# Every second chunk of an input matrix: the low half of a float32 split completed by an adding DMA instead of GpSimd

## The chip, the core and the metric

The kernel runs on one core of one Trainium2 chip. The metric is the device time of one execution in microseconds (us), given as the median of several runs. In the text, PE is TensorE, DVE is VectorE, ACT is ScalarE, POOL is GpSimd and SP is SyncE, which here only issues DMAs. "L120" is line 120 of the kernel before.

## The reference

One decoder block over 512 positions of 1024 channels, all in float32. Two token mixers (a gated depthwise convolution of 31 taps, and a gated linear recurrence) run on slices of one wide projection; their outputs are merged by sigmoid gates, and a SwiGLU layer follows. Cut to what matters:

```python
h = rmsnorm(x, norm1_g)                     # 512 x 1024
z = h @ w_in + b_in                         # w_in: 1024 x 6656
z_glu, z_rx, z_rg, z_ga, z_gb = split(z, [2048, 3328, 4608, 5632])
u = z_glu[:, :1024] * sigmoid(z_glu[:, 1024:])
u = silu(layernorm(causal_depthwise_conv(u, conv_dw_w, conv_dw_b)))
y_a = u @ conv_w_out + conv_b_out
xb = causal_depthwise_conv(z_rx, lru_conv_w, lru_conv_b)
y_b = (rg_lru(xb, ...) * gelu(z_rg)) @ lru_w_out
x = x + (sigmoid(z_ga) * y_a + sigmoid(z_gb) * y_b) @ w_mix_out
x = x + (silu(h2 @ ffn_w1) * (h2 @ ffn_w3)) @ ffn_w2       # h2 = rmsnorm(x, norm2_g)
return rmsnorm(x, norm_f_g)
```

The change concerns the second line alone, the product with `w_in`.

## The kernel before, in words

**Products.** Each float32 matrix is split into two parts in the rounded format float32r: a high part h = round(v) and a low part l = v - h. A product is then three TensorE matmuls, high by high, high by low and low by high (`mm3`). Operands lie channels by positions, so that a product of one 128-column chunk of `w_in` with all 512 positions is 8 blocks of 128 input channels times 3, that is 24 matmuls of 128x128 by 128x512, into one PSUM bank of 512 float32 per partition.

**Weight chunks.** `w_in` is cut into 52 chunks of 128 columns (512 KB each). The list `chunks` holds them, the ten gate chunks of the recurrence and all later weights in the order of use. `emit_chunk` makes one: it takes one of `RAW = 4` buffers (`raw`), lets SP load the chunk into it, takes one of `HL = 5` pairs of buffers (`hl`, high part in the first half, low part in the second), and splits. `weights(key)` emits chunks until `AHEAD = 4` beyond the one asked for. A `raw` buffer comes free when its split is done; an `hl` pair comes free when PE has read it.

**The split before.** `split_to` has ACT copy the chunk to the high part (L124, a rounding copy), and then POOL subtract it from the chunk into the low part (L120). For the first two `w_in` chunks VectorE does the rounding and POOL or VectorE the subtraction. Later weights (`lo=vec`) are subtracted by VectorE.

**The order.** `ORDER` lists the steps of this stage: `u` (two chunks, the gated convolution's input), `rx`, `rg`, `gb`, `ga` (one chunk each), `g` (two small products for the recurrence's gates, 8 or 12 matmuls, L868) and `r` (a scan, no matmul). So the first steps `u0 u1 rx0 rx1 gb0 rx2 u2` hold chunks 1 to 10. Beside these steps `run_beside` spreads the depthwise convolution on VectorE (L743, 240 instructions with one tap each) and then the layer norm, whose two column sums are a pair of matmuls each (`column_mean`, L754). `make_out_sums` lets POOL form sums of later weights (`ows`), which are loaded and stored through SP in the same stage. What each engine executes is its own queue in order; outside the blocks marked `manual_schedule` (the start of this stage and two short places later) a planner with estimated durations orders each queue at compile time, and semaphores hold the instructions at run time. PSUM has six banks for the products of this stage (`psum`); a bank comes free when ACT or VectorE has read it.

**Adding transfers before.** There is one such place: `f_sum` for two of the SwiGLU sums (L363), where POOL issues a DMA that adds one buffer onto another in SBUF.

Of the kernel before, what the change touches and what calls it, by code (L numbers as in the profile page):

```python
# [8 lines left out]
F32 = mybir.dt.float32  # L9
F32R = mybir.dt.float32r  # L10
AF = mybir.ActivationFunctionType
ALU = mybir.AluOpType

P = 128
# [12 lines left out]
ND = D // P  # L27
# [11 lines left out]
FEW, MANY = 32, 112  # L39

LAG = 12

# [43 lines left out]
def tile_block(ctx, tc, a, out):  # L88
# [25 lines left out]
    vec, act, pe, pool_e = nc.vector, nc.scalar, nc.tensor, nc.gpsimd  # L114
# [4 lines left out]
    def sub(eng, o, x, y):  # L119
        return eng.tensor_tensor(out=o, in0=x, in1=y, op=ALU.subtract)  # L120

    def split_to(h, l, full, eng, copy=act.copy):

        copy(h, full)  # L124
        if eng is vec and "tie" in newest:
            with tc.issue_after(newest["tie"]):
                last = sub(eng, l, full, h.bitcast(F32))
        else:
            last = sub(eng, l, full, h.bitcast(F32))
        if eng is pool_e:  # L130
            newest["sub"] = last.ins
        return h, l, last

    def split(name, full, eng, p_=None, copy=act.copy):
        p_ = p_ or pairt(name)
        return split_to(*p_, full, eng, copy)[:2]


    chunks = []
    held = {}  # L140
    emitted = [0]

    def wchunk(key, src, kt, cols, where="hl", lo=pool_e, after=None):
        chunks.append((key, src, kt, cols, where, lo, after))
# [13 lines left out]
    def emit_chunk(copy=act.copy, lo_by=None):  # L158
        if emitted[0] == GATES_AT:
            load_gates()  # L160
        key, src, kt, cols, where, lo, after = chunks[emitted[0]]
        emitted[0] += 1
        lo = lo_by or lo
        n = kt * cols
        if where == "made":
            raw = src()
        else:
            raw = raws.tile([P, 1024], F32, tag="raw", name=f"raw_{key}")
        rv = raw[:, :n]
        if where == "made":  # L170
            pass
        elif callable(src):
            src(raw)
        else:
            newest["load"] = nc.sync.dma_start(rv.rearrange("p (k n) -> p k n", k=kt), src).ins
        if where != "long":
            hl = hls.tile([P, 2, 1024], F32R, tag="hl", name=f"hl_{key}")
            h, l, _ = split_to(hl[:, 0, :n], hl[:, 1, :n], rv, lo, copy)
            if after:
                after(rv, h)  # L180
            held[key] = (h.rearrange("p (k n) -> p k n", k=kt), l.rearrange("p (k n) -> p k n", k=kt))
        else:
            held[key] = [
                split_to(longt(f"{key}h{i}", F32R), longt(f"{key}l{i}", F32R), rv[:, i * T : (i + 1) * T], lo)
                for i in range(2)
            ]

    def emit_to(n, copy=act.copy, lo_by=None):
        while emitted[0] < min(len(chunks), n):
            emit_chunk(copy, lo_by)  # L190
# [5 lines left out]

    w_in = a["w_in"][0].rearrange("(k p) n -> p k n", p=P)

    def w_in_chunk(m):
        wchunk(f"in{m}", w_in[:, :, m * P : (m + 1) * P], ND, P)  # L200

    GLU, RX, RG, GA, GB = 0, 16, 26, 36, 44
    pieces = gate_pieces()
# [8 lines left out]
    def load_gates():  # L212
      with tc.issue_after(newest["load"]):
        for gi, name in enumerate(("lru_wa", "lru_wx")):
            nc.sync.dma_start(gate_rows[:, gi, :], a[name][0].rearrange("h r n -> (h r) n"))
# [29 lines left out]
    for kind, j in ORDER:  # L245
        if kind == "g":
            gate_chunk(j)
        elif kind == "u":
            w_in_chunk(GLU + j)
            w_in_chunk(GLU + 8 + j)  # L250
        elif kind != "r":
            w_in_chunk({"rx": RX, "rg": RG, "gb": GB, "ga": GA}[kind] + j)
# [218 lines left out]
    def row_at(c):  # L471
        b = sum(c >= s_ for s_ in starts) - 1
        return b + (c - starts[b]) // P, (c - starts[b]) % P

    at, col, parts = 0, {}, []
    for name, n in ROWS:
# [4 lines left out]
        while done < n:  # L481
            m = min(n - done, P - row_at(at + done)[1])
# [189 lines left out]
    with tc.manual_schedule(engines={ET.PE, ET.Activation, ET.DVE, ET.SP}):  # L672
# [23 lines left out]
        _, ws, ps = early[0]  # L696
# [34 lines left out]
    def beside():  # L731
# [18 lines left out]
        def column_mean(name, tot, scale):  # L750

            ps = bank2(f"{name}p")
            for i, v in enumerate(tot):
                pe.matmul(ps, onesr, v, start=i == 0, stop=i == 1)  # L754
            act.activation(ps, ps, AF.Copy, scale=scale)
            return ps

        def pause(n):
            for _ in range(n):
                yield  # L760
# [6 lines left out]
        tot = split("lnms", tot, vec)  # L767
        yield from pause(LAG)
        mean = column_mean("lnm", tot, 1.0 / DC)
# [10 lines left out]
        tot = split("lnvs", tot, vec)  # L780
        yield from pause(LAG)
        rs = column_mean("lnv", tot, 1.0 / DC)
# [599 lines left out]
```

## Time and profile before

| | |
|---|---|
| median of 3 runs | 795.95 us (795.84 to 796.22) |
| span of the profiled execution, first to last instruction | 794.7 us, 1.25 us under the median |
| busy: PE | 786.6 us (99%), 4300 matmuls |
| busy: DVE, ACT, POOL | 688.9 us (87%), 473.8 us (60%), 221.9 us (28%) |
| granted TensorE clock | 1.00 throughout |
| DMA queues | 135.32 MB by SP's hardware queue, 1.05 MB by POOL's software queue |
| the 52 loads of `w_in` chunks | issued between 3.0 and 282.0 us, 512 KB each |

The profile gives for each instruction its engine, line, operands by name, start and duration, and what ended the engine's idle time before it. The stage of the change lies between some 25 and 320 us. The chain of work that ended last is followed back from the last instruction; where it stays on one engine, that engine was not waiting for another. DMA share is the mean busy share of the core's 16 DMA engines.

### The profile page before, as it was taken

What the parts mean: (1) busy time and instruction counts of PE and PEld (TensorE: products, weight loads), DVE (VectorE), ACT (ScalarE), POOL (GpSimd) and SP (SyncE); (2) the same over time, 40 slices, a digit from 0 to 9 for tenths busy, and PEclk for the clock granted to TensorE, in tenths of its full rate; (3) what the DMA queues carried; (4) which work ended last, traced back from release to release, by engine and by line L of the source; (5) the groups of instructions that cost most, each with busy time, mean ns of one, the idle gap of its engine ahead of it and who ended that gap; (6) DMA issues with size and microseconds to landing.
All of it is one profiled execution on the core that took longest, in us unless ns stands there. A gap on an engine that the chain in (4) does not pass through costs nothing.

```text
span 794.7 us, 12042 instructions
## 1 busy us (share of the span) xinstructions
PE 786.6 (99%) x4300; PEld 686.4 (86%) x4300; DVE 688.9 (87%) x1047; ACT 473.8 (60%) x695; POOL 221.9 (28%) x174
## 2 busy tenths in 40 slices
PE   8999999999999999999999999999999999999997
PEld 8888888888888888888888898999999999888886
DVE  6699899999989988786887889979888888989867
ACT  7645685987768855563335575545455555585544
POOL 1865766797666856030000000000000000000000
PEclk9999999999999999999999999999999999999999
DMA  7955646487564664359847545655333332686552
GB/s 209 247 145 145 193 139 206 121 247 208 170 206 138 206 189 119 129 192 276 271 159 247 173 133 159 182 152 164 114 108 107 106 106 81 200 287 201 186 172 106
DMA packets 184603, 137.14 MB, mean 173 GB/s; under 512 B 14259, under 2 KB 163167, under 8 KB 184543
## 3 DMA queue, kind: packets, MB, share of 16 engines
q1 hardware_dynamic: 184255, 135.32, 56.3%
q0 software_dynamic: 288, 1.05, 0.7%
q8 instruction: 34, 0.56, 0.3%
q14 instruction: 26, 0.21, 0.1%
HBM read 113.79 MB, written 18.64 MB: 167 GB/s over the span
## 4 chain that ended last, share of the span: by engine, by line
PE 92%; DMA 3%; DVE 3%; ACT 1%; issue 0%; SPq 0%; ACTq 0%; POOLq 0%; DVEq 0%
PE z L544 35%; PE or L1003 12%; PE yb L544 7%; PE ft L1141 7%; PE fa L1141 7%; PE ya L544 5%; PE mxr L1003 5%; PE fr L1141 3%; PE g L868 3%; PE fb L1141 2%; PE fe L1151 2%; PE f L544 1%; DMA raw_fb<-raw_fb 1%; PE fe L1152 1%; DMA raw_fb<-in_ffn_w_dram 1%; PE f L1175 1%
## 5 line engine op out<-in xcount | busy, mean ns | idle before, releaser
L743 DVE SCALAR_TENSOR_TENSOR cv<-u,par,cv 128x511 f32<-128x511 f32 (+19 forms) x240 | 162.4, 731 | 6.0 <-ACT cv L740 5.7
L120 POOL TENSOR_TENSOR hl_in<-raw_in,hl_in 128x1024 fp32r<-128x1024 f32 x50 | 121.1, 2427 | 73.7 <-ACT hl_in L124 67.8
L120 POOL TENSOR_TENSOR ows<-ows 128x256 f32<-128x256 f32 x66 | 56.5, 858 | 37.9 <-DMA ows<-in_ffn_w_dram 34.9
L124 ACT CAST hl_ft<-raw_fb 128x1024 fp32r<-128x1024 f32 x40 | 41.9, 1050 | 31.7 <-DVE raw_fb L365 14.8
L124 ACT CAST hl_in<-raw_in 128x1024 fp32r<-128x1024 f32 x50 | 52.0, 1043 | 12.7 <-PE z L544 6.6
L120 DVE TENSOR_TENSOR hl_ft<-raw_fb,hl_ft 128x1024 fp32r<-128x1024 f32 x40 | 48.6, 1220 | 9.4 <-ACT hl_ft L124 9.4
L363 POOL DMA_DIRECT2D raw_fb<-raw_fb x2 | 1.9, 928 | 158.1 <-DVE raw_fb L365 158.1
L120 DVE TENSOR_TENSOR hl_fb<-raw_fb,hl_fb 128x1024 fp32r<-128x1024 f32 x30 | 36.7, 1223 | 8.4 <-ACT hl_fb L124 8.0
L544 PE MATMUL z<-h10h,hl_in 128*128 128x512 f32 (+1 forms) x106 | 41.1, 388 | 0.2 <-DVE h10l L600 0.2
L544 PE MATMUL z<-h12h,hl_in 128*128 128x512 f32 (+1 forms) x106 | 40.6, 384 | 0.0
L544 PE MATMUL z<-h14h,hl_in 128*128 128x512 f32 (+1 forms) x106 | 40.6, 384 | 0.0
L544 PE MATMUL z<-h17h,hl_in 128*128 128x512 f32 (+1 forms) x106 | 40.6, 384 | 0.0
L544 PE MATMUL z<-h11h,hl_in 128*128 128x512 f32 (+1 forms) x106 | 40.6, 383 | 0.0
L544 PE MATMUL z<-h16h,hl_in 128*128 128x512 f32 (+1 forms) x106 | 40.6, 383 | 0.0
L544 PE MATMUL z<-h13h,hl_in 128*128 128x512 f32 (+1 forms) x106 | 40.6, 383 | 0.0
L544 PE MATMUL z<-h15h,hl_in 128*128 128x512 f32 (+1 forms) x106 | 40.6, 383 | 0.0
L365 DVE TENSOR_TENSOR raw_fb<-raw_fb,raw_fb 128x1024 f32<-128x1024 f32 x28 | 34.2, 1222 | 7.0 <-DMA raw_fb<-in_ffn_w_dram 6.7
L124 ACT CAST hl_fb<-raw_fb 128x1024 fp32r<-128x1024 f32 x30 | 31.4, 1047 | 8.6 <-PE mxr L1003 3.7
L124 ACT CAST hl_ob<-raw_ob 128x1024 fp32r<-128x1024 f32 (+1 forms) x23 | 23.3, 1015 | 19.6 <-PE or L1003 10.5
L120 DVE TENSOR_TENSOR hl_ob<-raw_ob,hl_ob 128x1024 fp32r<-128x1024 f32 (+1 forms) x23 | 27.1, 1176 | 6.3 <-ACT hl_ob L124 4.4
L1141 PE MATMUL ft<-hs_1h,hl_ft 128*128 128x256 f32 x160 | 30.4, 284 | 0.0
L124 ACT CAST hl_ot<-raw_ot 128x1024 fp32r<-128x1024 f32 (+1 forms) x17 | 17.5, 1027 | 17.8 <-PE or L1003 16.8
(1082 smaller groups left out, 2630.7 us busy)
## 6 DMA issues: line engine op xcount, KB each, us to landing
raw_in<-in_w_in_dram SPq DMA_DIRECT2D x52, 512.0 KB
raw_fb<-in_ffn_w_dram SPq DMA_DIRECT2D x96, 256.0 KB
ows<-in_ffn_w_dram SPq DMA_DIRECT2D x44, 256.0 KB
os<-ows SPq DMA_DIRECT2D x22, 512.0 KB
raw_ob<-in_ffn_w_dram SPq DMA_DIRECT2D x33, 256.0 KB
raw_ot<-os SPq DMA_DIRECT2D x33, 256.0 KB
raw_lo<-in_lru_w_out_dram SPq DMA_DIRECT2D x16, 320.0 KB
x<-in_x_dram SPq DMA_DIRECT2D x16, 256.0 KB
```

What stands on the lines that cost most here:

```text
L120: return eng.tensor_tensor(out=o, in0=x, in1=y, op=ALU.subtract)
L124: copy(h, full)
L363: pool_e.dma_start(out=q, in_=y, accum_op=ALU.add)
L365: vec.tensor_tensor(out=q, in0=q, in1=y, op=ALU.add)
L544: pe.matmul(ps, l, r, start=i == 0, stop=i == n - 1)
L743: vec.scalar_tensor_tensor(out=acc[c][:, s:], in0=u[c][:, : T - s], scalar=dw(c, s), in1=acc[c][:, s:], op0=ALU.mult, op1=ALU.add)
L868: pe.matmul(ps, l, r, start=k == 0, stop=k == len(mms) - 1)
L1003: pe.matmul(banks[i], l_[:, ts], r_, start=start and n == 0, stop=stop and n == 2, skip_group_check=again)
L1141: pe.matmul(ps[:, HALVES[i]], lw[:, 4 * i + c, :], rx_, start=not (again or i or c or m), stop=bool(i and c == 3 and m == 2), skip_group_c ...
L1151: pe.matmul(ps, h[:, 4 * i + c, :], both_[c], start=c == 0, stop=False, skip_group_check=True)
L1152: pe.matmul(ps[:, LO], l[:, 4 * i + c, :], xh, start=False, stop=c == 3, skip_group_check=True)
L1175: pe.matmul(plain_1[:, cs], l, r, start=k == 0 and m == 0, stop=k == ND - 1 and m == 2)
```

## The change

`w_in` chunks are counted as they are listed. Of the 52, those with an even number from 6 on (6, 8, ..., 52: 24 chunks) are split in another way: ACT writes the negated rounded chunk into the low part, POOL issues a DMA that adds the chunk onto it (so that the low part is v - round(v)), and ACT then rounds the chunk into the high part. The other 28 chunks are split as before.

```diff
+TRANSFERS_FROM = 6
...
+    def split_by_transfer(h, l, full):
+
+        act.activation(l, full, AF.Copy, scale=-1.0)
+        last = pool_e.dma_start(out=l.bitcast(F32), in_=full, accum_op=ALU.add)
+        act.copy(h, full)
+        return h, l, last
...
         if where != "long":
             hl = hls.tile([P, 2, 1024], F32R, tag="hl", name=f"hl_{key}")
-            h, l, _ = split_to(hl[:, 0, :n], hl[:, 1, :n], rv, lo, copy)
+            parts_ = hl[:, 0, :n], hl[:, 1, :n], rv
+            h, l, _ = split_by_transfer(*parts_) if lo == "transfer" else split_to(*parts_, lo, copy)
...
+    n_in = [0]
+
     def w_in_chunk(m):
-        wchunk(f"in{m}", w_in[:, :, m * P : (m + 1) * P], ND, P)
+        n_in[0] += 1
+        by_transfer = n_in[0] >= TRANSFERS_FROM and n_in[0] % 2 == 0
+        wchunk(f"in{m}", w_in[:, :, m * P : (m + 1) * P], ND, P, lo="transfer" if by_transfer else pool_e)
```

## The prediction

> **What bounds the kernel now.** I read the busy times, then the chain that ended last, then busy time by stretch.
>
> ```profile
> PE 786.6 (99%) x4300; PEld 686.4 (86%) x4300; DVE 688.9 (87%) x1047; ACT 473.8 (60%) x695; POOL 221.9 (28%) x174
> ```
>
> The chain in order of time (start, length, what; x counts matmuls):
>
> ```profile
> 25.24 43.59 PE z L544 x192
> ...
> 118.85 2.76 PE g L868 x12
> ...
> 134.34 21.78 PE z L544 x96
> 156.12 1.85 PE g L868 x8
> 157.96 21.78 PE z L544 x96
> ...
> 243.37 65.30 PE z L544 x288
> 308.68 0.45 PE lnmp L754 x2
> ...
> 374.86 25.16 PE ya L544 x111
> ```
>
> Busy us (and instructions) of PE, PEld, DVE, ACT, POOL, then granted clock, DMA share, GB/s:
>
> ```profile
> 0.00:25.00 25.00, 22.40 (x160) 21.43 (x161) 16.08 (x46) 19.52 (x45) 6.29 (x10) 1.00 0.81 226
> 25.00:320.00 295.00, 295.00 (x1302) 244.11 (x1301) 275.44 (x416) 202.27 (x256) 207.02 (x159) 1.00 0.60 176
> 700.00:795.00 95.00, 89.38 (x402) 73.95 (x400) 78.77 (x123) 53.62 (x87) 0.00 (x0) 1.00 0.56 180
> ```
>
> The reader is to see three things. In the whole stage of the change (25 to 320 us) PE is busy 295.00 of 295.00 us, and the chain never leaves it. PE idles 2.6 us before that stage and 5.6 us at the kernel's end, and no edited chunk is used in either. And a matmul goes at the same pace whether POOL works or not: 21.78/96 = 227 ns beside POOL, 25.16/111 = 227 ns in the ya stage, where POOL has no split to do. So work taken from POOL cannot shorten PE's row; the question is only whether a chunk, a PSUM bank or a column sum now comes late.
>
> **The change part by part.** Prices, from rows grouped by form, the queue table, a window of the only adding transfers, and two waits (total us, times, longest):
>
> ```profile
> L120 POOL TENSOR_TENSOR hl_in<-raw_in,hl_in 128x1024 fp32r<-128x1024 f32 x50 | 121.1, 2427 | 73.7 <-ACT hl_in L124 67.8 <-issue 2.9 <-DMA raw_in<-in_w_in_dram 1.2
> L124 ACT CAST hl_in<-raw_in 128x1024 fp32r<-128x1024 f32 x48 | 49.9, 1043 | 12.3 <-PE z L544 6.6 <-DMA raw_in<-in_w_in_dram 4.3 <-issue 1.1
> L124 ACT CAST hl_gate<-raw_gate 128x512 fp32r<-128x512 f32 x10 | 6.1, 614 | 7.3 <-POOL ows L120 3.2 <-POOL hl_in L120 2.3 <-PE z L544 1.8
> L624 ACT ACTIVATE x<-x,stats 128x512 f32<-128x512 f32 x2 | 1.4, 724 | 0.6 <-DVE stats L568 0.6
> L363 POOL DMA_DIRECT2D raw_fb<-raw_fb x2 | 1.9, 928 | 158.1 <-DVE raw_fb L365 158.1
> ```
>
> ```profile
> q0 software_dynamic: 288, 1.05, 0.7%
> ```
>
> ```profile
> DMA to landing us min/median/max: 4.7/5.3/6.0
> ```
>
> ```profile
> 498.00:506.00 8.00, 8.00 (x69) 8.00 (x68) 8.00 (x13) 5.07 (x8) 1.00 (x1) 1.00 0.49 108
> ```
>
> ```profile
> ACT hl_in L124 <- DMA raw_in<-in_w_in_dram: 4.7, 3, 3.8
> ```
>
> ```profile
> SPq L175 <- POOL hl_in L120: 38.7, 19, 6.5
> ```
>
> *POOL, removed:* 24 subtractions of 2.43 us, 58.2 us; *added:* 24 issues of 0.93 us, 22.3 us. POOL goes from 207.0 to some 171 busy us. It is not on the chain: gain nothing.
>
> *ACT, added:* one negating copy of 128x1024 for each chunk. No row shows it. Its like is L624, a scaled copy of 512 columns in 724 ns; 512 more columns cost 1043-614 = 429 ns in the rounding copies, so 1.15 us. Ends: 1.04 us (as the rounding copy) and 1.45 us (twice L624); I take 1.15, as L624 is the same kind of instruction. L624's row has no table load beside it, so none is counted. 24 x 1.15 = 27.6 us, ACT from 202.3 to 229.9 of 295 us. In sum it is hidden under PE; where it is not is worked out below.
>
> *DMA, added:* the two transfers of before took 0.7% of 794.7 us on 16 engines, 2.8 us each; 24 of them are 67 us, and the stage's share goes from 0.60 to 0.83. That leaves room on the average, less in bursts.
>
> *The chunk's own delay.* Before: 1.04 + 2.43 and 0.08 between them, 3.55 us. Now 1.15 + 0.93 + 5.3 = 7.4 us until the low part is there (landing counted from the issue's end, the worse reading); the high part's rounding runs beside the transfer. So the low part comes 3.8 us later, and the raw buffer comes free 3.8 us later. The load behind it waits that long in SP's queue, where such waits exist already (38.7 us in 19), and what stands behind it with it: the ext copies for the gates, the loads and stores of ows. ACT waited for raw_in only 4.7 us in all, because loads wait in full buffers for a free hl pair; 3.8 us come out of that reserve. For the ext copies one row: the last piece for a gate product is issued at 110.54, and the product begins at 118.85, 8.3 us for one copy.
>
> Now the chunks with the least time, from the timeline (start, length, [idle before it]):
>
> ```profile
> 26.18 1.99 ACT L124 CAST hl_in<-raw_in 128x1024 fp32r<-128x1024 f32 x2
> ...
> 139.41 0.62 ACT L124 CAST xb5h<-xb 128x512 fp32r<-128x512 f32 x1 [6.22 <-DVE xb L821]
> 139.94 1.05 ACT L124 CAST hl_in<-raw_in 128x1024 fp32r<-128x1024 f32 x1
> ...
> 152.99 1.05 ACT L124 CAST hl_in<-raw_in 128x1024 fp32r<-128x1024 f32 x1
> ...
> 178.29 0.59 ACT L124 CAST y2h<-z 128x512 fp32r<-128x512 f32 x1 [2.26 <-DVE z L906]
> ...
> 248.76 1.04 ACT L124 CAST hl_in<-raw_in 128x1024 fp32r<-128x1024 f32 x1
> ```
>
> ```profile
> 27.30 4.75 POOL L120 TENSOR_TENSOR hl_in<-raw_in,hl_in 128x1024 fp32r<-128x1024 f32 x2 [0.55 <-ACT hl_in L124]
> ...
> 141.06 2.99 POOL L120 TENSOR_TENSOR hl_in<-raw_in,hl_in 128x1024 fp32r<-128x1024 f32 x1 [6.72 <-ACT hl_in L124]
> ...
> 154.12 2.81 POOL L120 TENSOR_TENSOR hl_in<-raw_in,hl_in 128x1024 fp32r<-128x1024 f32 x1
> ...
> 249.88 2.40 POOL L120 TENSOR_TENSOR hl_in<-raw_in,hl_in 128x1024 fp32r<-128x1024 f32 x1 [4.57 <-ACT hl_in L124]
> ```
>
> ```profile
> 110.54 0.53 SPq L848 DMA_DIRECT2D ext3l<-xb4l  x1
> ```
>
> A chunk is 24 matmuls, 5.44 us, and its third matmul (0.45 us in) is the first to need a low part. By ORDER the 96 matmuls from 134.34 are rx6, rg1 and the two chunks of u5; the second of these, chunk 24, begins at 134.34 + 16.33 = 150.67 and needs the low part at 151.12. ACT rounds it at 139.94. Now: negated by 141.1, issued by 142.0 (POOL was idle), landed at 147.3: 3.8 us to spare. Chunk 26 (gb3) is the second of the 96 from 157.96: needed at 163.85. ACT, busy without a gap since 139.41, comes 1.15 us later to it: 154.14, negated 155.3, issued 156.2, landed 161.5: 2.3 us to spare, the least of all. Chunk 42 (gb7), the fourth from 243.37, is needed at 260.14: 248.76, 249.9, 250.8, landed 256.1: 4.0 us. Chunk 6, the first by transfer, is rounded at 27.1, issued at some 30.6 behind POOL's work, landed at 35.9, needed at 25.24 + 16.33 + 0.45 = 42.0.
>
> So the landing time decides: chunk 26 makes PE wait from 7.6 us on, 24 from 9.1, 42 from 9.3. The row's 5.3 us were measured at a DMA share of 0.49; here it is higher:
>
> ```profile
> 25.00:35.00 10.00, 10.00 (x47) 8.29 (x46) 4.67 (x19) 5.94 (x7) 8.36 (x4) 1.00 1.06 260
> ...
> 145.00:155.00 10.00, 10.00 (x46) 8.29 (x45) 9.94 (x16) 9.79 (x14) 8.67 (x9) 1.00 0.38 111
> 155.00:165.00 10.00, 10.00 (x45) 8.25 (x45) 10.00 (x16) 9.90 (x14) 9.11 (x7) 1.00 0.64 192
> 165.00:175.00 10.00, 10.00 (x46) 8.29 (x45) 9.27 (x15) 9.89 (x14) 9.71 (x9) 1.00 0.90 261
> ```
>
> Lower end 4.7 us; upper end 8.1, if the 2.8 us of engine time double beside loads. At 5.3 PE waits 0; at 8.1 it waits 0.5 us, at chunk 26. I take 0.25. [...] The two transfers before ran beside loads at a share of 0.49 and do not decide it.
>
> **Sum:** -0 (POOL) + 0.25 (chunk 26) = +0.25 us: the profiled span from 794.7 to 794.95, the median, 1.25 us above it, from 795.95 to **796.2 us**. Changes under 0.2% (1.6 us) I call no change, about what a measurement of this kernel can tell.
>
> **The rivals.**
>
> *A. Landings of 12 us,* twice the longest seen, because software transfers and loads crowd (0.90 of the engines from 165 to 175 us before the change, 1.06 at 25 to 35). Then chunk 6 lands at 42.6, 0.6 us late; chunk 24 at 154.0 against 151.12 + 0.6, 2.3 late; chunk 26 at 168.2 against 163.85 + 2.9, 1.5 late; chunk 42 at 262.8 against 260.14 + 4.4, in time. Together 4.4 us on 795.95: 800.4 us. Against it: the share 0.38 at 145 to 155, and no landing over 6.0. It decides from some 9.5 us, where chunks 26 and 24 together cost 1.9 us.
>
> *B. ACT's backlog.* From 139.41 to some 176 ACT has no gap (9.79, 9.90, 9.89 of 10), and chunks 24, 26, 28 and 30 fall there: 4 x 1.15 = 4.6 us late before the gap at 178.29. PE's banks are freed by ACT, or by DVE behind ACT. With no slack PE would wait 4.6 us, with 1.6 us of it 3.0: 799.0 us. For it: those windows. Against it: DVE is as full there (9.94, 10.00), and ACT itself had waited 6.22 us for it, so DVE more than ACT sets when banks are freed. It decides from a slack under 3 us.
>
> *C. The planner's queues come out otherwise.* This stage is not ordered by hand, and new durations can move any instruction. The place with a number is the layer norm's first sum:
>
> ```profile
> L120 DVE TENSOR_TENSOR lnmsl<-lnmt,lnmsh x1: 1160/1160/1160, 304.6 to 304.6; 128x512 fp32r<-128x512 f32 x1
> ```
>
> It ends at 305.8, and PE needs it with the second matmul from 308.68, some 3.1 us later. Five negating copies put ahead of it on ACT (5 x 1.15 = 5.8 us) would make PE wait 2.7 us: 798.7 us.
>
> *D. Faster.* DVE is 93% busy in the stage, and some of it is waiting for POOL:
>
> ```profile
> L120 DVE TENSOR_TENSOR xb9l<-xb,xb9h 128x512 fp32r<-128x512 f32 x1 | 2.3, 2337 | 0.0
> L120 DVE TENSOR_TENSOR y7l<-z,y7h 128x512 fp32r<-128x512 f32 x1 | 0.7, 694 | 0.0
> ```
>
> An equal operation takes 694 ns with one input in PSUM and up to 2337 with both in SBUF, 1.6 us more, less than one POOL subtraction. [...] Half the subtractions gone frees a few us of DVE. But the end moves only if PE's idle time does: 5.6 us in the last 95, which this stage does not feed. If a shifted queue saved 2 us of them: 794.0 us.
>
> **How the numbers follow.** No change to be measured, as summed: 0.60. A 0.12, B 0.12, C 0.10: slower, 0.34. D 0.06. The likeliest gives 796.2, its own range 795.7 to 797.0. For 8 in 10 I reach from 795.2 to 800.5: this leaves out D and half of A, 0.12, and some of the likeliest's own edge.
>
> **What would show it.** Right: PE busy 295 of 295 us in the stage; 24 POOL issues near 0.9 us, and landings under 7.6; the negating copy near 1.15 us; ACT near 230, POOL near 171 us, DMA share near 0.83. Wrong: gaps in PE before z at chunk 24, 26 or 42 with the DMA as releaser (A), with ACT or DVE as releaser at 140 to 180 us (B), before lnmp (C), or fewer than 5.6 idle us after 700 (D). A negating copy that brings table loads, or an issue that holds POOL far above 0.93 us, would void the sum.

## The result, and the profile after

The changed kernel takes **807.8 us** (median of 4 runs, 806.5 to 810.7) against 796.0 (795.8 to 796.2): 1.0151 times as long, 95% interval 1.0139 to 1.0163. It is slower by 11.8 us where no change was forecast (796.2, range 795.2 to 800.5). The profiled execution took 806.5 us, the shortest of the four, with a span of 804.5 against 794.7; so 9.8 of the 11.8 us are seen in the profile. The medians and ratios of this document are those of fast executions; one execution of a later experiment (`from14`) took 1313.9 us at a mean granted clock of 0.557 and is left aside.

The busy times of the changed kernel:

```profile
PE 789.8 (98%) x4300; PEld 686.8 (85%) x4300; DVE 688.0 (86%) x1047; ACT 498.7 (62%) x721; POOL 183.7 (23%) x174
```

The parts cost about what they were said to cost: ACT 24.9 us more, POOL 38.2 less, and PE's work is the same. Its new operations, by form, and the landing times of the 24 transfers:

```profile
L142 ACT ACTIVATE hl_in<-raw_in 128x1024 fp32r<-128x1024 f32 x24 | 25.3, 1053 | 2.1 <-PE z L557 1.2 <-DMA raw_in<-in_w_in_dram 0.9
DMA to landing us min/median/max: 4.5/6.3/8.0
```

The time went where PE waits. Two names recur: g5, g6 and so on are the small gate products, and the ext copies gather, from a neighbouring `xb`, the rows that such a product also needs; some are made by ACT, the others by SP's DMAs. PE's waits in the changed kernel (total us, times, longest); in the kernel before none of these three exists:

```profile
PE g L881 <- DMA ext6h<-xb7h: 3.2, 1, 3.2
PE g L881 <- ACT ext L856: 2.1, 1, 2.1
PE z L557 <- DVE xb L893: 1.3, 1, 1.3
```

By stretch (busy us and instructions of PE, PEld, DVE, ACT, POOL; granted clock, DMA share, GB/s), after:

```profile
120.00:180.00 60.00, 56.61 (x241) 45.98 (x241) 57.70 (x88) 48.86 (x62) 33.81 (x33) 0.97 0.74 193
180.00:245.00 65.00, 61.67 (x265) 50.23 (x264) 57.59 (x87) 45.86 (x56) 36.08 (x36) 0.97 0.85 228
```

PE is full from 25 to 120 and from 245 to 320 us, so all that the stage loses is lost here; in shorter slices of the same view, between 140 and 195 us, mostly in these four:

```profile
155.00:160.00 5.00, 2.87 (x13) 2.13 (x12) 5.00 (x8) 4.94 (x9) 2.24 (x3) 1.00 0.52 144
160.00:165.00 5.00, 5.00 (x17) 3.92 (x16) 5.00 (x9) 4.97 (x7) 3.00 (x2) 0.66 0.89 199
...
185.00:190.00 5.00, 1.67 (x4) 1.07 (x4) 4.79 (x8) 1.28 (x3) 4.08 (x5) 0.83 0.76 251
190.00:195.00 5.00, 5.00 (x20) 3.97 (x19) 1.28 (x3) 4.65 (x7) 0.78 (x2) 0.83 0.97 277
```

From 160 to 165 PE is busy for all 5 us and does 17 matmuls, where a slice at full clock has 24. The trace dates the lower clock: it stands at 0.50 for 3.4 us behind the wait for ACT and for 3.4 us behind the wait for ext6h, as two windows at these places show:

```profile
161.00:164.40 3.40, 3.40 (x9) 2.63 (x8) 3.40 (x6) 3.37 (x4) 2.40 (x2) 0.50 0.98 230
188.30:191.70 3.40, 3.30 (x7) 2.33 (x8) 1.55 (x3) 1.36 (x2) 2.32 (x4) 0.51 0.62 176
```

At half the clock each of the two costs PE some 1.7 us. So the stage's account is this. The chain of work has, in the changed kernel:

```profile
24.32 43.59 PE z L557 x192
...
318.62 0.64 PE lnmp L767 x2
```

That is 294.30 us between the two points, and 283.44 before (25.24 to 308.68 in the prediction's rows): 10.86 us more. The three waits are 6.6 of it and the two stretches at half the clock 3.4; the other 0.9 are what the instructions around the waits lose. After lnmp the two executions differ by 0.1 us.

**Where each wait comes from.** The first two begin on ACT and DVE. The first, for a PSUM bank, ends when DVE has read the bank, before and after:

```profile
143.57 0.68 DVE L880 SCALAR_TENSOR_TENSOR xb<-g,xb 128x512 f32<-128x512 f32 x1
```

```profile
144.83 0.69 DVE L893 SCALAR_TENSOR_TENSOR xb<-g,xb 128x512 f32<-128x512 f32 x1
```

It is 1.26 us later, as long as PE waits; xb5, some instructions ahead of it on DVE, was late by as much. For the second wait, ACT's queue ahead of the ext copies that g5 needs, in the kernel before (start, length, instruction):

```profile
149.46 1.12 ACT L890 ACTIVATE mu<-th 128x512 f32<-128x512 f32 x2
...
152.48 0.61 ACT L124 CAST xb6h<-xb 128x512 fp32r<-128x512 f32 x1
...
155.33 0.62 ACT L843 CAST ext<-xb6h 32x512 fp32r<-32x512 f32 x1
```

The same in the changed kernel:

```profile
140.65 0.62 ACT L125 CAST xb5h<-xb 128x512 fp32r<-128x512 f32 x1 [8.39 <-DVE xb L834]
141.18 1.05 ACT L142 ACTIVATE hl_in<-raw_in 128x1024 fp32r<-128x1024 f32 x1
...
151.65 0.60 ACT L903 ACTIVATE mu<-th 128x512 f32<-128x512 f32 x1
152.27 1.28 ACT L918 ACT_TABLE_LOAD   x1
153.57 0.66 ACT L918 ACTIVATE z<-z,par 128x512 f32<-128x512 f32 x1
154.25 1.28 ACT L903 ACT_TABLE_LOAD   x1
...
156.08 0.61 ACT L125 CAST xb6h<-xb 128x512 fp32r<-128x512 f32 x1
...
158.79 0.62 ACT L856 CAST ext<-xb6h 32x512 fp32r<-32x512 f32 x1
```

The last ext copy ended at 155.95 and PE first used it at 156.63: 0.7 us to spare. Now the rounding of xb6 is 3.6 us later: xb5 was rounded 1.2 later, one negating pass adds 0.95 (instructions on ACT overlap a little), and the planner has put the Gelu of rg1 (L918) between the two square roots (L903), with one table load more ahead of xb6, 1.4 us.

Why xb5 was late already, from DVE's timelines, before and after, and POOL's after:

```profile
122.30 0.33 DVE L233 CAST hl_gate<-raw_gate 32x256 fp32r<-32x256 f32 x1
```

```profile
121.39 1.80 DVE L246 CAST hl_gate<-raw_gate 32x256 fp32r<-32x256 f32 x1
```

```profile
120.65 2.40 POOL L121 TENSOR_TENSOR hl_in<-raw_in,hl_in 128x1024 fp32r<-128x1024 f32 x1
```

The same cast takes 1.5 us longer and ends with POOL's subtraction (123.05). It began 0.9 us earlier than before and ended 0.6 later; one tap of the convolution more ahead of xb5 (0.65 us) makes the rest of xb5's 1.2. In both traces it ended 0.14 us behind the POOL instruction in which it began: now the subtraction of 2.40 us, of which 1.66 us were left, and it took 1.80; before, a shorter one for ows that ended at 122.49, of which 0.19 us were left, and it took 0.33. So less POOL work in all made one collision, because POOL came to its subtraction at another moment.

The third wait begins in SP's queue. Before:

```profile
163.15 0.60 SPq L452 DMA_DIRECT2D os<-ows  x1
...
166.77 1.23 SPq L437 DMA_DIRECT2D ows<-in_ffn_w_dram  x2
...
174.22 0.54 SPq L848 DMA_DIRECT2D ext6h<-xb7h  x1
```

After, and what SP waited for longest between 163 and 182 us:

```profile
167.56 0.61 SPq L465 DMA_DIRECT2D os<-ows  x1
174.17 1.25 SPq L450 DMA_DIRECT2D ows<-in_ffn_w_dram  x2
...
180.67 1.96 SPq L861 DMA_DIRECT2D ext6h<-xb7h  x1
```

```profile
SPq L450 <- DMA os<-ows: 5.9, 1, 5.9
```

A transfer of the change was issued at 167.47, and the store right behind it took some 6 us to land; the ows loads wait for it, and the ext copies for xb7 stand in the queue behind them, issued 6.4 us later than before. Once issued, the first packet of ext6h moved after 5.3 us, where before it took 1.6; another transfer of the change had been issued at 178.0. So ext6h came 10.1 us later, and PE itself 4.6. Before, ext6h had landed at 178.1 us and PE loaded it at 180.0: 1.9 us to spare (1.6 for ext6l), too little for the difference. SP is not alone in this, as xb7 itself was rounded 6.2 us later on ACT:

```profile
169.51 0.62 ACT L124 CAST xb7h<-xb 128x512 fp32r<-128x512 f32 x1
```

```profile
175.69 0.61 ACT L125 CAST xb7h<-xb 128x512 fp32r<-128x512 f32 x1
```

It was ready some 4 us before SP came to its copies; with SP on time, the copies would have waited for ACT instead.

### The profile page after: what moved, and what is told of

The parts are those of the page before. It is cut to its first block, busy times and chain, and to the rows that moved or that the text cites. A ratio compares the mean times of both kernels' runs of the same rounds, so it can differ in the third digit from the quotient of the medians.

```text
span 804.5 us, 12106 instructions
## 1 busy us (share of the span) xinstructions
PE 789.8 (98%) x4300; PEld 686.8 (85%) x4300; DVE 688.0 (86%) x1047; ACT 498.7 (62%) x721; POOL 183.7 (23%) x174
## 4 chain that ended last, share of the span: by engine, by line
PE 86%; DVE 8%; ACT 3%; DMA 2%; issue 1%; SPq 0%; ACTq 0%
PE z L557 26%; PE or L1016 12%; PE ft L1154 7%; PE yb L557 7%; PE fa L1154 6%; PE fr L1154 6%; PE ya L557 5%; PE mxr L1016 5%; DVE cv L756 4%; PE fb L1154 2%; PE f L557 2%; PE g L881 2%; PE fe L1164 2%; PE fe L1165 1%; DMA ext6h<-xb7h 1%; PE f L1188 1%
## 5 line engine op out<-in xcount | busy, mean ns | idle before, releaser
L756 DVE SCALAR_TENSOR_TENSOR cv<-u,par,cv 128x511 f32<-128x511 f32 (+15 forms) x240 | 162.2, 729 | 9.4 <-ACT cv L753 9.3
L121 POOL TENSOR_TENSOR hl_in<-raw_in,hl_in 128x1024 fp32r<-128x1024 f32 x26 | 62.4, 2399 | 65.2 <-ACT hl_in L125 65.0
L125 ACT CAST hl_in<-raw_in 128x1024 fp32r<-128x1024 f32 x26 | 27.1, 1042 | 10.1 <-PE z L557 6.5
L143 POOL DMA_DIRECT2D hl_in<-raw_in x24 | 21.1, 879 | 40.2 <-ACT hl_in L142 35.9
```

The costliest lines, as they stand in the source:

```text
L143: last = pool_e.dma_start(out=l.bitcast(F32), in_=full, accum_op=ALU.add)
L756: vec.scalar_tensor_tensor(out=acc[c][:, s:], in0=u[c][:, : T - s], scalar=dw(c, s), in1=acc[c][:, s:], op0=ALU.mult, op1=ALU.add)
```

## The experiments

Each is an edit of the changed kernel unless it says otherwise. "Stage" is the time from the first z product to lnmp, both by their first matmul: 297.9 us before, 308.7 after.

**Which half?** The ACT pass alone, with POOL adding the chunk in the transfer's place:

```diff
-        last = pool_e.dma_start(out=l.bitcast(F32), in_=full, accum_op=ALU.add)
+        last = pool_e.tensor_tensor(out=l, in0=full, in1=l.bitcast(F32), op=ALU.add)
```

> The 24 chunks keep the second pass on ACT (the negated rounding into the low part), but POOL adds the chunk onto it with a subtraction's twin instead of a transfer; nothing is left out. Theory A (ACT: the 24 passes of 1.05 us, 25 us in all, come between the small copies that the gates and banks wait for, among them the ext copies that PE waited 2.1 us for): most of the loss stays, 802 to 808 us. Theory H (hold: a transfer holds its raw buffer for 6.3 us, the memset of a gate chunk on POOL waited 14.3 us in 3 for such buffers, and DVE behind it 4.0 us): no transfer, so 795.5 to 797.5. Theory D (crowding: the transfers' 13 MB stretch other transfers, the ext copy that PE waited 3.2 us for took 7.5 us): 795.5 to 797.5.

Measured 800.2 us, ratio 1.0051 (1.0036 to 1.0066). Of the three waits one is left, and the clock falls once behind it (0.94 from 155 to 160 us and 0.72 from 160 to 165, together what 3.4 us at 0.50 give):

```profile
PE g L881 <- ACT ext L856: 2.1, 1, 2.1
```

The transfer alone (ACT rounds once, POOL negates the high part into the low part, then the transfer):

```diff
-        act.activation(l, full, AF.Copy, scale=-1.0)
+        act.copy(h, full)
+        pool_e.tensor_scalar(out=l, in0=h.bitcast(F32), scalar1=-1.0, scalar2=None, op0=ALU.mult)
         last = pool_e.dma_start(out=l.bitcast(F32), in_=full, accum_op=ALU.add)
-        act.copy(h, full)
```

> The 24 chunks keep the adding transfer, but ACT rounds once, as before, and POOL negates the high part into the low part ahead of the transfer; nothing is left out. ACT's work is that of the kernel before. Theory A: 795.5 to 798. Theory H: the hold is as long or longer, so 803 to 811. Theory D: 803 to 811.

Measured 806.4 us, ratio 1.0125 (1.0095 to 1.0155). Its waits are those of SP's queue and of a late bank; the ACT wait is gone:

```profile
PE z L557 <- DVE xb L893: 3.0, 2, 2.0
PE g L881 <- DMA ext6l<-xb7l: 2.7, 1, 2.7
PE g L881 <- DMA ext6h<-xb7h: 1.4, 1, 1.4
```

So the ACT part costs about 4 us (the wait of 2.1 and the 1.7 of the clock make 3.8) and the transfers about 10. Together that is more than the 11.8 of the change; that their waits cover each other in part would explain it, but no run shows it.

**Every transfer, or a few places?** `TRANSFERS_FROM = 14`, so that the first four chunks by transfer go:

> Transfers from chunk 14 on instead of 6: 20 transfers, none before 60 us, where DVE in the changed kernel lost 5 us of work (33.7 busy us from 25 to 70 against 39.0 before). Theory H: DVE keeps its lead, the wait of z for DVE goes and the later waits shrink: 797 to 803 us. Theory A: chunk 26's pass ahead of the ext copies stays, and PE waits there: 801 to 806. Theory D: the ext copy at 180 us is stretched as before: 801 to 806.

809.3, 810.3 and 816.0 us (interval 1.0173 to 1.0257): not better. PE waits 5.0 us for ext6h, 2.8 in two for banks and 1.6 for ACT's copies, the last alone less than in the changed kernel. The early transfers are not the cause. `TRANSFERS_FROM = 34`, 10 transfers:

> Transfers from chunk 34 on: 10 of the 24, all later than the two tight places at 158 and 180 us. Tight places: 795.5 to 797.5 us. General crowding: some 10/24 of the loss, 799 to 802, with a wait for ext8 near 228 us.

796.6 us, 1.0004 (0.9994 to 1.0013), none of the three waits, although the transfers land no sooner (5.4/6.3/8.6 us). And the three chunks around the places split as before (`and n_in[0] not in (26, 28, 30)`):

> The changed kernel with chunks 26, 28 and 30 split as before: 21 transfers. Theory of two tight places (ACT's ext copies at 158 us behind the pass of chunk 26; the ext copies of xb7 at 180 us beside the transfer of chunk 30): both waits go, 2.1 + 3.2 us and the slow clock behind them: 797 to 801 us. Theory of a general backlog: 804 to 808.

801.9 us, 1.0075 (1.0059 to 1.0092). The wait for xb7 is gone and the two others stand (2.1 us for ACT's ext copies, 1.2 for the bank), and the mean granted clock of the profile is 1.000.

A cost of each transfer is ruled out: ten late ones cost nothing, and three taken out at the right place gave back 6 of 11.8 us.

**The raw buffer held, or the engines crowded?** Gate chunks with a raw buffer of their own (and one 2 KB slot less elsewhere), so that no memset on POOL waits for a transfer:

```diff
-            raw = raws.tile([P, 1024], F32, tag="raw", name=f"raw_{key}")
+            raw = gateraws.tile([P, 512], F32, tag="graw", name=f"raw_{key}") if after else raws.tile([P, 1024], F32, tag="raw", name=f"raw_{key}")
```

> The changed kernel, but gate chunks get a raw buffer of their own (128x512), so that POOL's memset no longer waits for a transfer to land; one buffer of the 59 long ones is given up for the space. Theory H: the 14.3 us of POOL's memset and the 4.0 us of DVE behind it go, and with them the wait of z for DVE (1.3 us) and some of the two later ones: 797 to 803 us. Theory A and theory D: the ext copies on ACT and the stretched transfer stay, 804 to 810.

811.9 us, 1.0201 (1.0186 to 1.0217). The stage is as long as in the changed kernel (308.6); 4.8 us more lie behind it, where PE waits 2.5 us ahead of the second column sum; the mean granted clock of 0.994 is a loss of 4.9 us in 810.4, of which the stage has 3.4. That the missing slot makes this is likely, but not shown. The z wait went, but the wait for xb7 grew from 3.2 to 5.6. Two tries at one suspect alone, made from the split of before, went astray. The first added 24 copies of 1 MB in device memory:

> The kernel before, and beside it, at the places of the 24 transfers, POOL issues a plain 1 MB copy inside HBM that nothing waits for: ACT's work, the split and the hold of the raw buffers are those of before, only the DMA engines are fuller. Theory D (crowding stretches the ext copies that the gate products wait for): PE waits for ext6h or ext6l near 180 us, 799 to 808 us. Theory H (buffers held): 795.5 to 797.

861.1 us, 1.0802 (1.0776 to 1.0828). Nothing tied the copies to their chunks, so they ran from 1.3 to 99.9 us in a heap; PE waited 27.4 us at the start. This shows that a crowd can cost much, not that this one did. The second copied one column of each raw buffer out, to hold it longer:

> The kernel before, and at the places of the 24 transfers POOL issues a copy of one column (512 bytes) of the raw buffer to HBM, so that the buffer comes free some 3 us later, with no crowding and no further ACT pass. Theory H: loads behind it in SP's queue come later and with them the ext copies, PE waits near 180 us, 799 to 806 us. Theory D: 795.5 to 797.

809.6 us, 1.0166 (1.0151 to 1.0181). But the copies came ahead of other work in POOL's queue before their data was there, and POOL waited:

```profile
POOL copied L149 <- DMA raw_in<-in_w_in_dram: 54.0, 16, 6.5
```

The run says what stopping POOL costs, not what holding a buffer does. The clean versions came later. A transfer of 512 KB from an unused buffer behind each of the 24 subtractions, and its control, the kernel before with the two slots less that this buffer takes:

```diff
-SLOTS, SHORT, GATES = 59, 5, 6
+SLOTS, SHORT, GATES = 57, 5, 6
...
+        with tc.issue_after(last.ins):
+            pool_e.dma_start(out=copied[n_copied[0] % 4][:, :], in_=spare)
```

> A control for the next run: the kernel before with two 2 KB slots less, which the next run needs for a buffer. Nothing of the split is changed. Waits, if any, should fall after the stage (from 309 us on), where the queues differ; the stage itself (first z product to lnmp, 297.9 us in the kernel before) should be unchanged within 0.5 us.

> The split of the kernel before with those two slots less, and after each of the same 24 subtractions POOL issues one 512 KB transfer from a buffer that nothing else uses to device memory: transfers of the change's number and size, no ACT pass, no raw buffer held, no low part that waits. Theory 'crowding': in the stretch 140 to 190 us ext copies and stores land later, PE waits for ext copies of xb7 or xb9, and the stage is 4 to 10 us longer than in the control. Rival 'holding the raw buffers': the stage is at most 1 us longer. The issue on POOL (0.9 us each behind the subtraction) counts against both; if it decides, POOL is the releaser.

Control: 796.9 us, 1.0010 (1.0001 to 1.0020), against the expectation with a stage of 304.8, since products of a later step moved ahead of lnmp; it is compared only with its own kind. With the transfers: 797.8 us, 1.0023 (1.0014 to 1.0033), a stage of 306.1, no wait for an ext copy. What makes that stage 1.3 us longer is not shown: PE waited 1.5 us for h10l, 1.2 in the control, and the granted clock is 1.00 from 120 to 320 us in both, 0.998 over the whole of each profile. The queue table shows the limit of this test, the changed kernel's row first:

```profile
q0 software_dynamic: 3744, 13.63, 9.0%
```

```profile
q0 software_dynamic: 3744, 13.63, 4.9%
```

As many packets and bytes as the change, at 4.9% of the engines' time where the adding transfers take 9.0%. Plain transfers of that size cost 0.9 us in all here, hardly more than the intervals can tell; adding ones were not tried without a raw buffer. A fifth raw buffer tells it from the other side (`RAW = 5`, the same two slots less), for the transfer alone and for the change:

> The kernel with the transfer part alone (ACT rounds once, POOL negates, the adding transfer completes the low part; it measured 806.4 with 4 raw buffers), with a fifth raw buffer and two 2 KB slots less for it; its control with those slots less measured 796.9. The adding transfers, their crowd on the engines and POOL's work stay. Theory 'holding the raw buffer until the transfer has landed stops SP's queue and POOL': with a buffer more the loads no longer wait, and the time falls to 797 to 800. Rival 'crowding by the adding transfers, 9 per cent of the engines' time instead of 4.9': 804 to 807, PE again waiting for ext copies of xb7.

> The changed kernel (807.8) with a fifth raw buffer and two 2 KB slots less. Theory 'holding': the wait for the ext copies of xb7 (3.2 us) goes or falls under 1 us, and what is left is the ACT part, 4 us over the control's 796.9: 799 to 802. Rival 'crowding': that wait stays above 2 us, 806 to 809.

806.0 us, 1.0144 (1.0113 to 1.0175), and 809.1 us, 1.0164 (1.0149 to 1.0179): nothing gained, against the theory of holding as I had put it. In the second the wait for ext6h grew from 3.2 to 6.7 us. POOL and SP in the first of the two:

```profile
174.03 0.52 POOL L236 MEMSET raw_gate<- 128x512 f32 x1 [5.40 <-DMA hl_in<-raw_in]
```

```profile
182.06 0.58 SPq L861 DMA_DIRECT2D ext6h<-xb7h  x1
```

With five buffers in turn, another chunk gives its buffer to the gate chunk, and its transfer had been issued just before, at 167.7. POOL's memset waits 5.4 us for the landing, POOL's sums of ows come behind it, SP's store behind these, and the ext copies behind the store: PE waits 5.3 us for ext6h, although xb7 was rounded only 1.5 us later than before (171.0 against 169.5) and the copies were issued 7.8 later. In the changed kernel the memset at that place did not wait, and it was the store that landed late. So the tight place is fixed, SP's queue ahead of the ext copies of xb7, and what fills it changes from version to version. How much of it is holding and how much crowding stays open.

**The three places one by one.** The Gelu of rg1 queued behind the second square root, as it was before:

```diff
+        if j == 1:
+            recur(2)
+            recur(3)
+            with tc.issue_after(newest["mu3"]):
+                act.activation(ps, ps, AF.Gelu_apprx_tanh, bias=b_in(RG + j))
...
-            recur(j)
+            if j not in (2, 3):
+                recur(j)
```

> The changed kernel with one edit: the Gelu of rg1 (L918 there) is queued on ACT behind the square root of r3, as it stood in the kernel before. On ACT nothing else moves; one table load (1.28 us) less stands ahead of the rounding of xb6. Theory 'tight places' (each of three small delays in a place with little slack makes one wait of PE): the wait of g5 for the ext copies (2.1 us) shrinks by 1.3 to about 0.8 us, the other two stay at 1.3 and 3.2, and the time falls from 807.8 to some 804.5 to 806.5, by more where the granted clock no longer falls after that wait. Rival 'the negating passes themselves are the whole delay': the wait stays at 2.1, 807.8.

812.3 us, 1.0197 (1.0182 to 1.0212):

```profile
PE g L881 <- DMA ext6h<-xb7h: 9.3, 1, 9.3
PE z L557 <- DVE xb L893: 1.3, 1, 1.3
PE g L881 <- ACT ext L856: 0.7, 1, 0.7
```

The wait for ACT shrank by 1.4 us, as one table load should. The next place then lost 6.1 us more, and the time rose: on ACT the rounding of a chunk, with that of xb7 behind it, waited for the chunk's load:

```profile
174.40 1.05 ACT L125 CAST hl_in<-raw_in 128x1024 fp32r<-128x1024 f32 x1 [4.77 <-DMA raw_in<-in_w_in_dram]
```

So xb7 was rounded 3.7 us later than in the changed kernel (179.3) and its ext copies issued 3.3 later, while PE, with the shorter wait behind it, came there 2.8 us sooner. A load in SP's queue that ACT's earlier backlog had hidden was now the late one. The same edit where there are no transfers:

> The kernel with only the ACT part of the change (negating pass kept, POOL adds the chunk to it, no transfer; it measured 800.2), and the Gelu of rg1 queued behind the square root of r3 on ACT, so that one table load (1.28 us) less stands ahead of the rounding of xb6. Theory 'the ACT part's 4 us are one wait, made by the other order of the queue': the wait of g5 for ext (2.25 us) falls to 0.5 to 1.0, the granted clock stays at 1.00, and the time is 796.3 to 797.5. Rival 'the passes themselves': 799.5 to 800.5.

799.8 us, 1.0051 (1.0035 to 1.0066), runs from 798.2 to 802.5. The wait fell to 0.7 us in the profile here too, but two new ones for xb7 (0.6 and 0.3) came, and the median is no better than without the edit, where the expectation's rival had it (799.5 to 800.5). In the profiled execution, the shortest, the granted clock is 1.00 from 120 to 320 us. That the table load makes 1.4 of the wait's 2.1 us is shown, here and in `pair_order`; that it makes the ACT part's 4 us is not. Chunk 10 split as before, whose raw buffer held up a memset for 7.0 us and DVE behind POOL for 4.0:

> The changed kernel with chunk 10 split as before (23 transfers). Its raw buffer goes to the second gate chunk, whose memset on POOL waited 7.0 us for the transfer, and DVE waited 4.0 us for POOL at 48.7 us. The queue of DVE is the same as in the changed kernel, row by row. Theory 'tight places, held buffer': DVE's wait falls to about 1 us or under, DVE is 3 us ahead at 130 us, the z wait for a PSUM bank (DVE xb, 1.3 us) goes, and the time falls from 807.8 to some 805.5 to 806.7. Rival 'crowding or ACT late': that z wait stays, 807.8.

807.9 us, 1.0147 (1.0132 to 1.0162). DVE's wait fell from 4.0 to 1.1, and the z wait stood at 1.3: DVE waited for ACT instead, and lost its 1.5 us at the cast. My reason for that wait fell. The ext copies of xb7 from ACT's queue:

```diff
-                    nc.sync.dma_start(ext[key][d][at0 : at0 + nr, :].bitcast(F32), src[k])
+                    (nc.scalar if i == 7 else nc.sync).dma_start(ext[key][d][at0 : at0 + nr, :].bitcast(F32), src[k])
```

> The changed kernel with the four ext copies of xb7 issued from ACT's queue instead of SP's. Theory 'they come late because they stand behind SP's other transfers, in its queue (about 1 us) and then in its ring behind a load and an adding transfer (first packet 5.3 us after the issue, 1.6 before the change)': first packet under 3 us after the issue, issue at once after the low part, and the wait of g6 (3.2 us) goes or is under 1 us; 801.5 to 805. Rival 'the 16 engines are full at that time, whatever the ring': first packet again some 5 us after the issue, the wait above 2 us, 806 to 808.

809.4 us, 1.0163 (1.0148 to 1.0178). The first packet of ext6h now moved 2.0 us after its issue and the wait fell from 3.2 to 2.0 (1.4 and 0.6), but the issues held ACT:

```profile
186.21 1.28 ACT L912 ACT_TABLE_LOAD   x1 [8.03 <-DMA ext6h<-xb7h]
```

The wait moved to another queue. All three relieved at once (chunks 10, 18, 26, 28 and 30 as before, and the Gelu's place):

> The changed kernel with all three places relieved: chunks 10, 18, 26, 28 and 30 split as before (19 transfers), and the Gelu of rg1 behind the square root of r3. Theory 'tight places': no PE wait over 1.2 us is left between 25 and 309 us, the granted clock stays at 1.00, and the time is 796 to 798.5. Rival 'a cost spread over all transfers' (0.5 us each, 11.8/24): 19 of them give 805.

798.8 us, 1.0035 (1.0022 to 1.0047), with 19 transfers still there. Of the three waits, 0.4 us is left for ACT's ext copies, none for xb7, and the first:

```profile
PE z L557 <- DVE xb L893: 1.2, 1, 1.2
```

And chunk 24 as before as well, so that no negating pass stands ahead of the Tanh of g4, which a bank waits for:

> The kernel with the three places relieved (798.8), and chunk 24 split as before as well, so that no negating pass (1.05 us) stands ahead of the Tanh of g4 on ACT; 18 transfers are left. Theory 'tight places': the last wait there (z for a PSUM bank that DVE frees late, 1.4 us) falls to 0.5 or less, and the time is 796.3 to 797.5. Rival 'the wait comes from DVE alone, whose cast of a gate chunk stood 1.5 us behind POOL's subtraction': the wait stays above 1 us, 798.3 to 799.2.

797.9 us, 1.0022 (1.0012 to 1.0032). The z wait is 0.6 now, with DVE's cast still at 1.80 us: the pass made half of that wait, the cast is the likely other half. Of the 11.8 us, some 10 are gone with 18 of 24 transfers kept. No version beat the kernel before.

## Why the prediction was wrong

**Right.** The low parts were never late: PE never waited for hl_in, and chunk 26, given 7.6 us from the issue's end, was in time. POOL, ACT and DMA sums came as worked out: the negating pass took 1.05 us (taken: 1.15), the issue 0.88 (0.93), ACT 24.9 us (27.6). Landings went up to 8.0 us, median 6.3, where 5.3 was taken, and no chunk was late by it. The doubling of the 2.8 us of engine time beside loads, which gave the upper end of 8.1 us and so the 0.25 us of the sum, was an estimate, and no run shows it: in the changed kernel 9.0% of 804.5 us for 26 transfers is again 2.8 us each. The longest landing is near 8.1 all the same, and the median nearer to the 5.3 measured before. PE's order did not change, and lnmp was not late.

**Wrong, first: SP's queue.** The step "For the ext copies one row ... 8.3 us for one copy" judged all ext copies by those for g3. Those for g6 had 1.9 us (1.6 for ext6l). The 3.8 us of delay that the same paragraph passed into SP's queue would have been too much for them, and more came: their issue was 6.4 us later and the first packet another 3.7, with PE itself 4.6 later. This was the largest wait (3.2 us, up to 9.3 in the experiments).

**Second: ACT's copies.** The ext copies for g5 are made by ACT itself, ended 0.7 us before their use, and stand behind ACT's full stretch, which rival B named (139 to 176 us). B was right in place and releaser; but it looked for late banks, where ACT's own copies were late by more (2.1 us against 1.3), and it was priced alone, at 3.0 us, and doubted because "DVE is as full there".

**Third: the planner.** Rival C looked for the harm at lnmp. The queue did come out otherwise, at rg1, and brought a table load of 1.28 us where 0.7 us were to spare. That no table load is counted for the negating copy was right; the table load came from a neighbour.

**Fourth: waits were taken one at a time.** A, B and C were each given 0.10 to 0.12 as if only one could happen, and the range ended at 800.5. They lie in one stretch, in which DVE and ACT have no gap, and came together; 1.3, 2.1 and 3.2 us make 6.6. **And the clock** was taken as 1.00 throughout: the 3.4 us of the two falls to 0.50, and some 0.9 around the waits, had no term at all.

## What to carry to other kernels

An engine at 100% on the chain says that nothing is late now, not by how much: before moving work between the other engines, list every operand that reaches it through an in-order queue and take the smallest time to spare, not one example. In a stretch where two or three engines are full, count the late places together, with the clock that PE can lose after each (here 3.4 us at 0.50 after two of the three). Moving work off an idle engine (POOL here) has no gain to set against that.

## What the hardware showed

The granted clock fell after waits of PE. In the changed kernel it stood at 0.50 for 3.41 us after the wait of 2.1 us and again after that of 3.2, and did not fall after that of 1.3; the two falls begin at 161.03 and 188.33 us. In slices of 5 us the clock of the experiments comes to as much, 3.4 or 3.5 us at 0.50, in each fall of `act_only`, `ext7_act` and `dma_only`, to 6.8 or 6.9 in six profiles with waits of 3.8 to 6.7 us (`skip10`, `hold_only`, `from14`, `dma_raw5`, `gate_own`, `raw5`) and to 10.3 after the 9.3 us of `pair_order`. Leaving `crowd_only` out, all nine waits of 2.7 us or more between 25 and 320 us brought a fall; of the eight of 2.0 to 2.1 us four did, in `after`, `act_only`, `ext7_act` and `dma_only`, and those in `gate_own`, `raw5`, `skip10` and `skip26_30` did not; nor did those of 1.2 to 1.3. What divides the four from the four is not shown.

The changed kernel's four executions took 806.5 and 807.0 us at a mean granted clock of 0.995, 808.5 at 0.993 and 810.7 at 0.991. A clock lower by 0.002 is 1.6 us in 805, about what one fall of 3.41 us costs (1.7). That such falls make this difference fits, but only the first of the four has a profile.

A 32x256 cast on DVE that began inside a subtraction on POOL with 1.66 us of it left took 1.80 us; before, with 0.19 us left, 0.33. In the kernel before, the subtraction for xb9l on DVE (213.35 us), which the prediction has under D, began inside one of POOL's (212.74 to 215.13) and took 2.34 us; that for xb8l (186.44), beside none, took 0.68. And an adding transfer within SBUF took nearly twice the engine time of a plain store to device memory with the same packets and bytes: 9.0% of an 804.5 us span against 4.9% of 798.1, both with the two transfers that were there before.
